# The down product of a conv-gated feed-forward network: Strassen-Winograd sums against eight open PSUM banks, and absorbed attention weights moved behind the token rows

## The chip, the cores and the metric

One core of one Trainium2 chip. The metric is device microseconds of the whole kernel, the median of the runs of one build. The engines are TensorE (PE), VectorE (DVE), ScalarE (ACT), GpSimd (POOL) and the queue SyncE (SP), which issues nearly all of this kernel's DMAs.

## What is computed

A decoder trunk of two layers over 1024 tokens of width 1024, in fp32. Layer 0 mixes tokens by an RWKV-7 recurrence, layer 1 by sparse attention (an indexer picks 256 keys per token); each is followed by a feed-forward network and both by a layer norm over a scaled residual. The parts that the change touches:

```python
def conv_ffn(x, w_up, conv_w, conv_b, w_down):       # w_down: (2816, 1024)
    u = x @ w_up
    u = sum(up[:, j:j + S] * conv_w[j] for j in range(CONV_W)) + conv_b
    gate, val = jnp.split(u, 2, axis=-1)
    return (jax.nn.silu(gate) * val) @ w_down
...
x = layer_norm(DN_ALPHA * x + f, ln_g[i, 1], ln_b[i, 1])

def dsa_attention(x, w_in, ..., w_uq, w_uk, ...):
    h = x @ w_in                                     # 456 columns
    ...
    q = (c_q @ w_uq).reshape(B, S, H, QK_HEAD)
    q_abs = jnp.einsum('bthd,hdc->bthc', q_b, w_uk)  # w_uq and w_uk are multiplied ahead ("absorbed")
```

## The kernel before, in words

`trunk` (line 1937) makes four generators: `rwkv` (307), `ffn` for layer 0 (884), `dsa` (1270), `ffn` for layer 1. `drive` (1945) steps two neighbours in turn, one `yield` each, so that the end of one phase and the start of the next stand side by side. Within that, the framework's scheduler sets each engine's order; engines wait for one another by semaphores, and buffers of a pool's tag are taken in turn.

An fp32 product is made of three fp32r matmuls: `split` (line 50) writes a cast `hi` (line 54, ScalarE) and the remainder `lo` (line 60, POOL or VectorE), and `mm3` (lines 63 to 67) multiplies hi by hi, and each hi by the other's lo. A matmul of the down product has 128 rows and 512 columns, and its result is one PSUM bank of 128 x 512.

The feed-forward network multiplies up, makes the gated convolution (`gated`, lines 1028 to 1049, mostly VectorE), and stores the hidden rows, transposed, as `hd` in DRAM: 22 blocks f of 128 hidden columns by 1024 tokens. The last two blocks are gated inside the down part.

The **down product** (lines 1124 to 1266) works on pairs of blocks by the seven products of Strassen and Winograd, named 11, 12, S1 to S4 and 22. The pairs are put into groups (cuts 0, 3, 6, 8, 10 in layer 0, and 0, 3, 6, 9 in layer 1). `d_load` (1135, 1136) loads hidden rows and weight rows of a pair; `d_op` (1143) makes the sums and differences `q` and `raw` on VectorE (908, 1147) and splits them into `dh` and `dl`; `down` does, for each of four token tiles tt, three matmuls per pair of the group into a bank `dn`. `add_to` (1164) reads the bank after every product step and adds it to `acc` in SBUF, 196 times over both layers (1166). Blocks left over, two in layer 0 and four in layer 1, are plain products `dt` (tiles `to`, `tr`) per token tile and half of the columns, read at line 1260, and followed by the layer norm and the store of the tile (`norm_store`, line 149 the store).

The attention's first steps are: `uq` and `uk` are loaded (1316, 1319) and multiplied in eight groups of fp32 matmuls of 64 rows (`wqk`, 1326); each result is copied (1330, ScalarE), split (`wqkh`, `wqkl`) and stored for later (1334). The input weights `w_in` come as eight blocks through two raw tiles (1339) and are split into `win`. Each token tile is then loaded (`x_load`, 1310, two halves `xr`), transposed (`x_T`, 1357, `pt`), cast, and projected (`w_in`, `win`: 24 matmuls of 456 columns), two tiles behind the loads. Then come the transposes `ht`, the indexer's weights (`wr`, `wq`, line 1456), its product `qi`, and the query blocks; a table `toep` of 1 MB (1466) takes the buffer of `uq`. Six shared buffers `u` hold `xr`, `uk`, `wqk`, `wqkl` and the normalised projections.

Of the kernel before, what the change touches and what calls it, by code (L numbers as in the profile page):

```python
# [7 lines left out]
F32 = mybir.dt.float32  # L8
# [6 lines left out]
D = 1024  # L15
# [868 lines left out]
def ffn(k, layer, src, dst):  # L884
# [239 lines left out]
    NPAIR = NF // 2  # L1124
    cuts = [0, 3, 6, 8, 10] if layer == 0 else [0, 3, 6, 9]
    groups = [range(a, b) for a, b in zip(cuts, cuts[1:])]
    in_P = (0, 3, 4, 8, 9) if layer == 0 else (0, 3, 6, 8)
    tail = range(2 * cuts[-1], NF)
    acc = []
    R = {}  # L1130

    def d_load(p):
        r = R[p] = dict(raw=big("raw", P_ if p in in_P else L_, (128, 8, 512), F32))
        raw = r["raw"]
        nc.sync.dma_start(raw[:, 0:4].rearrange("p (f a) c -> p f (a c)", f=2), hd[p].rearrange("f p c -> p f c"))
        nc.sync.dma_start(
            raw[:, 4:8].rearrange("p (f a) c -> p f (a c)", f=2),
            k.w_down[layer, p * 256 : (p + 1) * 256, :].rearrange("(f p) c -> p f c", p=128),
        )

    def d_op(p, n, pool, lo_eng):

        r = R[p]
        raw = r["raw"]
        if n == "S1":
            q = r["q"] = sm("q")
            nc.vector.tensor_tensor(q[:, 0], raw[:, 1], raw[:, 3], ALU.add)  # L1147
            sub(q[:, 1], raw[:, 5], raw[:, 4])
        elif n == "S2":
            q = r["q"]  # L1150
            sub(q[:, 0], q[:, 0], raw[:, 0])
            sub(q[:, 1], raw[:, 7], q[:, 1])
        elif n == "S3":
            sub(raw[:, 1:6:4], raw[:, 0:8:7], raw[:, 1:6:4])
        elif n == "S4":
            sub(raw[:, 2], raw[:, 2], r["q"][:, 0])
        elif n == "22":
            sub(raw[:, 6], raw[:, 6], r["q"][:, 1])
        hi, lo = t4("dh", F32R, pool, (128, 2, 512)), t4("dl", F32R, pool, (128, 2, 512))
        r[n] = hi, lo  # L1160
        at = {"11": slice(0, 5, 4), "12": slice(2, 7, 4), "S3": slice(1, 6, 4), "S4": slice(2, 8, 5), "22": slice(3, 7, 3)}
        split(k, raw[:, at[n]] if n in at else r["q"], hi, lo, "a", lo_eng)

    def add_to(hf, tt, ch, ps, first):
        o = acc[hf][:, tt, 512 * ch : 512 * ch + 512]
        nc.vector.scalar_tensor_tensor(o, o, ALPHA if first else 1.0, ps, ALU.mult, ALU.add)  # L1166

    B_ = {}

    def down(gi, n, tt):  # L1170
        new = n in ("11", "12", "S1")
        x = n in ("11", "S2", "S3", "22")
        if new:
            B_[x, tt] = bank("dn", PX if x else PY)
        ps = B_[x, tt]
        tsl = slice(128 * tt, 128 * tt + 128)
        for j, p in enumerate(groups[gi]):
            hi, lo = R[p][n]
            mm3(
                k, ps, (hi[:, 0, tsl], lo[:, 0, tsl]), (hi[:, 1], lo[:, 1]), new and j == 0,  # L1180
                n in ("12", "S4", "22") and j == len(groups[gi]) - 1, skip_group_check=True,
            )
        hf, ch = {"11": (0, 0), "12": (0, 0), "S1": (1, 1), "S2": (0, 1), "S3": (1, 1), "S4": (0, 1), "22": (1, 0)}[n]
        add_to(hf, tt, ch, ps, gi == 0 and n in ("11", "S1", "S2", "22"))

    for p in groups[0]:
        d_load(p)
    for hf in range(2):
        a = big("acc", L_, (128, 4, 1024), F32)
        acc.append(a)  # L1190
        for tt in range(4):
            nc.sync.dma_start(a[:, tt], src[(4 * hf + tt) * 128 : (4 * hf + tt + 1) * 128, :])
    ng = len(groups)
    dsteps = [(gi, n) for gi in range(ng) for n in ("11", "12", "S1", "S2", "S3", "S4", "22")]
    done = set()

    def d_ops(j):
        if j < len(dsteps) and j not in done:
            done.add(j)
            gi, n = dsteps[j]  # L1200
            for i, p in enumerate(groups[gi]):
                d_op(p, n, N_ if i == 2 else P_, CFG["dl0"][3 * j + i] if j < 3 else "v" if i == 2 and n in ("11", "12", "S4") else "p")

    hs = []

    def tail_op(f):

        if layer == 1 and f == NF - 1:
            room = [t4("to", F32R, N_) for _ in range(4)]
        else:  # L1210
            room = big("to", L_, (128, 4, 1024))
            room = [room[:, i] for i in range(4)]
        for i, ap in enumerate((hd[f // 2][f % 2], k.w_down[layer, f * 128 : (f + 1) * 128, :])):
            raw = t4("tr")
            nc.sync.dma_start(raw, ap)
            split(k, raw, room[2 * i], room[2 * i + 1], "a", "p")
        hs.append(room)

    late = [NF - CFG["gl"] + i for i in range(CFG["gl"])]
    for j, (gi, n) in enumerate(dsteps):  # L1220
        for x in CFG["ga"] if j == 0 else "":
            if x == "g":
                gated(late.pop(0))
            else:
                d_ops(int(x))
        d_ops(j)
        if n == "11" and gi + 1 < ng:
            for p in groups[gi + 1]:
                d_load(p)
        d_ops(j + 1)  # L1230
        if j == 0:
            while late:
                gated(late.pop(0))
        if gi == ng - 1 and n in ("S2", "S3", "S4") and (i := ("S2", "S3", "S4").index(n)) < len(tail):
            tail_op(tail[i])
        for tt in range(4):
            down(gi, n, tt)
    if len(tail) > 3:
        tail_op(tail[3])
    lnw = []  # L1240
    for z in range(2):
        if layer == 0:
            lnw.append(L_.tile([128, D], F32, name=f"lnw{z}"))
        else:
            lnw.append(sm("lnw").rearrange("p a b -> p (a b)"))
        i = B_LN + 4 * layer + 2 + z
        nc.sync.dma_start(lnw[z], k.bvec[i : i + 1, :].to_broadcast([128, D]))
    if layer == 0:
        pools.close(P_, N_, PY)
        yield  # L1250
    for tt in range(8):
        tsl = slice(128 * tt, 128 * tt + 128)
        r = [acc[tt // 4][:, tt % 4, 512 * ch : 512 * ch + 512] for ch in range(2)]
        sums = L_.tile([128, 2], F32, name="lns", tag="lns", bufs=2)
        for ch in range(2):
            cs = slice(512 * ch, 512 * ch + 512)
            ps = bank("dt")
            for i, (a, b, c, d) in enumerate(hs):
                mm3(k, ps, (a[:, tsl], b[:, tsl]), (c[:, cs], d[:, cs]), i == 0, i == len(hs) - 1)
            nc.vector.scalar_tensor_tensor(  # L1260
                r[ch], r[ch], 1.0, ps, ALU.mult, ALU.add, accum_out=sums[:, ch : ch + 1]
            )
# [713 lines left out]
```

## Time and profile before

| | us |
|---|---|
| median of 3 runs | 3173.01 (3172.37 to 3178.31) |
| profiled execution, own time | 3170.01 |
| its span, first to last instruction | 3168.0 |
| down product of layer 0, first `dn` to last `dt` | 1437.8 to 1729.6 |
| start of the attention up to the indexer's product | to 1784.65 |
| down product of layer 1 | 2893.1 to 3158.9 |

| engine | busy us | share of the span |
|---|---|---|
| PE | 2834.0 | 89% |
| DVE | 2463.5 | 78% |
| POOL | 1528.7 | 48% |
| ACT | 1368.9 | 43% |

The mean granted clock of TensorE is 0.937 of full speed. The spans of the table of engines overlap, so a share says little about one stage; the stages are read one by one, by their stretch of the span. "Idle before" in a row is what ended the engine's idle time ahead of it.

### The profile page before, as it was taken

To read this page: it belongs to the slowest core of one execution; us is meant where nothing else is said; L and a number is where in the kernel's file an instruction comes from. 1 tells how busy PE (TensorE), PEld (TensorE's weight loads), DVE (VectorE), ACT (ScalarE), POOL (GpSimd) and SP (SyncE) were. 2 spreads that over 40 slices of the span, in tenths; PEclk is the share of its full clock that TensorE was granted. 3 is DMA by queue.
4 is the path that set the end of the run, shared out by engine and by line. 5 is a ranking of instruction groups with operands and counts; after the bars stand their busy time and mean duration, and the time that the engine had idled before them with its cause. 6 is when DMAs were issued, how large, how long until landed. Compare 5 with 4: busy or idle time off the path is not lost. (4 is left out here: it accounts for less than half of the span.)

```text
span 3168.0 us, 41686 instructions
## 1 busy us (share of the span) xinstructions
PE 2834.0 (89%) x15032; PEld 2217.4 (70%) x15032; DVE 2463.5 (78%) x3911; ACT 1368.9 (43%) x2353; POOL 1528.7 (48%) x987
## 2 busy tenths in 40 slices
PE   7789998898988999997888888889998899998798
PEld 3577576786866777775667765667776677777577
DVE  6776776768576888889786699995675888888965
ACT  4433243322233544443224487784363444444231
POOL 3525045140246666666677222212214666666766
PEclk9889998898998999998998989899999999999899
DMA  6645435344162222244115221113224222225212
GB/s 214 246 152 195 142 121 199 134 148 146 64 201 89 80 80 80 80 143 189 41 40 173 102 90 37 34 40 115 77 66 151 60 80 80 80 81 206 80 53 93
DMA packets 235232, 354.87 MB, mean 112 GB/s; under 512 B 17194, under 2 KB 110762, under 8 KB 234642
## 3 DMA queue, kind: packets, MB, share of 16 engines
q1 hardware_dynamic: 221202, 327.04, 31.6%
q10 hardware_dynamic: 13824, 25.17, 2.2%
q8 instruction: 118, 1.93, 0.3%
q14 instruction: 88, 0.72, 0.1%
HBM read 248.99 MB, written 103.15 MB: 111 GB/s over the span
## 5 line engine op out<-in xcount | busy, mean ns | idle before, releaser
L60 POOL TENSOR_TENSOR wo<-wr,wo 128x512 fp32r<-128x512 f32 x220 | 414.3, 1907 | 289.4 <-ACT wo L54 289.4
L1039 DVE SCALAR_TENSOR_TENSOR cv<-u,vec,cv 128x1023 f32<-128x1023 f32 (+1 forms) x176 | 348.0, 1995 | 52.9 <-ACT cv L1034 51.2
L65 PE MATMUL dn<-dh 128*128 128x512 f32 x532 | 220.3, 414 | 67.8 <-DVE acc L1166 67.8
L60 POOL TENSOR_TENSOR dl<-raw,dh 128x1024 fp32r<-128x1024 f32 x82 | 220.2, 2708 | 102.2 <-ACT dh L54 96.7
L65 PE MATMUL p<-xT,wo 128*128 128x512 f32 x528 | 213.1, 404 | 27.8 <-ACT u L1023 18.2
L66 PE MATMUL dn<-dl,dh 128*128 128x512 f32 x532 | 218.1, 410 | 14.3 <-DVE dl L60 7.5
L1671 POOL TENSOR_TENSOR cm<-sc,toep 128x256 f32<-128x256 f32 x96 | 75.7, 795 | 298.1 <-DVE mn L1687 229.7
L1034 ACT ACTIVATE cv<-u,vec 128x1024 f32<-128x1024 f32 x88 | 109.5, 1244 | 250.2 <-DVE u L1028 249.6
L67 PE MATMUL dn<-dh,dl 128*128 128x512 f32 x532 | 217.0, 408 | 0.0
L67 PE MATMUL p<-xT,wo 128*128 128x512 f32 x528 | 208.8, 395 | 2.9 <-POOL wo L60 2.9
L66 PE MATMUL p<-xT,wo 128*128 128x512 f32 x528 | 208.5, 395 | 3.0 <-DVE xT L60 3.0
L1166 DVE SCALAR_TENSOR_TENSOR acc<-acc,dn 128x512 f32<-128x512 f32 x196 | 131.0, 680 | 86.3 <-PE dn L67 86.3
L60 POOL TENSOR_TENSOR wo<-S,wo 128x512 fp32r<-128x512 f32 x88 | 173.3, 1987 | 30.0 <-ACT wo L54 25.7
L54 ACT CAST dh<-raw 128x1024 fp32r<-128x1024 f32 x95 | 94.8, 1047 | 199.6 <-issue 81.1
L65 PEld LDWEIGHTS dn<-dh 128*128 128x128 f32 x532 | 106.3, 200 | 98.5 <-DVE acc L1166 42.2
L60 POOL TENSOR_TENSOR wl<-wr,wh 128x512 fp32r<-128x512 f32 x56 | 76.3, 1363 | 181.7 <-ACT wh L54 109.1
L65 PEld LDWEIGHTS p<-xT,wo 128*128 128x128 f32 x528 | 100.7, 191 | 65.4 <-ACT u L1023 33.0
L65 PE MATMUL p<-x,wo 128*128 128x512 f32 x352 | 138.9, 394 | 3.4 <-DVE x L60 3.0
L54 ACT CAST wo<-wr 128x512 fp32r<-128x512 f32 x220 | 127.2, 619 | 27.3 <-POOL wo L60 18.6
L67 PE MATMUL p<-x,wo 128*128 128x512 f32 x352 | 138.4, 393 | 0.0
L66 PE MATMUL p<-x,wo 128*128 128x512 f32 x352 | 138.4, 393 | 0.0
L66 PEld LDWEIGHTS dn<-dl,dh 128*128 128x128 f32 x532 | 106.5, 200 | 38.4 <-DVE dl L60 8.4
(412 smaller groups left out, 8552.0 us busy)
## 6 DMA issues: line engine op xcount, KB each, us to landing
wr<-in_w_up_dram SPq DMA_DIRECT2D x88, 512.0 KB, 5.9
hd<-cv SPq DMA_DIRECT2D x44, 512.0 KB, 3.4
raw<-hd SPq DMA_DIRECT2D x19, 1024.0 KB, 5.0
raw<-in_w_down_dram SPq DMA_DIRECT2D x19, 1024.0 KB, 7.6
wr<-in_w_wo_dram SPq DMA_DIRECT2D x68, 256.0 KB, 2.9
wr<-in_w_rkv_dram SPq DMA_DIRECT2D x48, 256.0 KB, 4.3
kept_w<-wh ACTq DMA_DIRECT2D x48, 256.0 KB, 3.5
kept_w<-wl SPq DMA_DIRECT2D x48, 256.0 KB, 3.0
```

The source lines that it names most:

```text
L54: nc.scalar.copy(hi, raw)
L60: eng.tensor_tensor(lo, raw, f32(hi), ALU.subtract)
L65: mm(ps, lhs[0], rhs[0], start=start, stop=False, **kw)
L66: mm(ps, lhs[0], rhs[1], start=False, stop=False, **kw)
L67: mm(ps, lhs[1], rhs[0], start=False, stop=stop, **kw)
L1034: nc.scalar.activation(o, u, AF.Identity, bias=k.vec[:, cb : cb + 1], scale=k.vec[:, cw[2] : cw[2] + 1])
L1039: nc.vector.scalar_tensor_tensor(o[:, d:], u[:, : 1024 - d], k.vec[:, cw[j] : cw[j] + 1], o[:, d:], ALU.mult, ALU.add)
L1166: nc.vector.scalar_tensor_tensor(o, o, ALPHA if first else 1.0, ps, ALU.mult, ALU.add)
L1671: (nc.vector if CFG["cm"][h4] == "v" else nc.gpsimd).tensor_tensor(cm[:, :near], mk, toep[g][:, h % 8, 256 - near :], ALU.add)
```

## The change

The down product is a plain one. Tokens are done in two halves hf of 512. For each pair p of hidden blocks `d_prep`, two steps ahead, loads half of the hidden rows (`hr`) and two blocks of the weights (`dr`), and splits all three; the weights are loaded and split anew for the second half. `d_mm` does six matmuls into each of eight banks (four token tiles by two halves of the columns), which stay open over all 11 pairs, 48 matmuls a step. The last two pairs are done bank by bank in `d_end`, which reads the bank once (line 1167 of the new file), and `d_norm` norms and stores the tile. The second half's last banks are taken in turn with the attention's first steps.

In the attention, the absorbed weights become a function `absorb`, called after the loop over token tiles; the rows of tiles 0 and 1 are loaded first; `w_in` comes through five raw tiles, two of tag `qr` and three of tag `ph`. Of the diff, the removed down product is cut out; it stands above.

```diff
-    cuts = [0, 3, 6, 8, 10] if layer == 0 else [0, 3, 6, 9]
...
+    NPAIR, LAST = NF // 2, 2
+    ops, hold, lnw, sums, rows = {}, {}, [], {}, {}
+    def d_prep(hf, p):
+        late = hf == 1 and p >= NPAIR - LAST
+        hr = t4("hr")
         nc.sync.dma_start(
+            hr.rearrange("p (f c) -> p f c", f=2), hd[p][:, :, 512 * hf : 512 * hf + 512].rearrange("f p c -> p f c")
         )
+        if late:
...
+            h = hold["h"][:, i], hold["h"][:, i + 1]
+        else:
+            h = t4("hh", F32R), t4("hl", F32R)
+        w = big("wd", L_ if late or layer and (hf * NPAIR + p) % 2 else P_, (128, 4, 1024))
+        split(k, hr, *h, "a", "p" if layer and hf and p < 4 else "v")
+        for f in range(2):
+            wr = t4("dr", pool=N_)
+            nc.sync.dma_start(wr, k.w_down[layer, (2 * p + f) * 128 : (2 * p + f + 1) * 128, :])
+            split(k, wr, w[:, 2 * f], w[:, 2 * f + 1], "a", "p")
+        ops[hf, p] = *h, w
+
+    def d_mm(ps, hf, p, tt, ch):
+        hh, hl, w = ops[hf, p]
+        for f in range(2):
+            ts = slice(512 * f + 128 * tt, 512 * f + 128 * tt + 128)
+            cs = slice(512 * ch, 512 * ch + 512)
             mm3(
+                k, ps, (hh[:, ts], hl[:, ts]), (w[:, 2 * f, cs], w[:, 2 * f + 1, cs]), p == f == 0,
+                p == NPAIR - 1 and f == 1,
             )
+    def d_end(ps, hf, tt, ch):
+        for p in range(NPAIR - LAST, NPAIR):
+            d_mm(ps, hf, p, tt, ch)
...
+        nc.vector.scalar_tensor_tensor(
+            r, r, ALPHA, ps, ALU.mult, ALU.add, accum_out=sums[hf, tt][:, ch : ch + 1]
+        )
+    def d_norm(hf, tt):
...
+    steps = [(hf, p) for hf in range(2) for p in range(NPAIR)]
+    for s in steps[:2]:
+        d_prep(*s)
+    for f in range(NF - CFG["gl"], NF):
+        gated(f)
+    order = [(ch, tt) for ch in (1, 0) for tt in range(4)]
+    for i, (hf, p) in enumerate(steps):
+        if i + 2 < len(steps):
+            d_prep(*steps[i + 2])
+        if p == 0:
+            bk = {x: bank("dn", PX if x[0] == 0 else PY) for x in order}
+        if p < NPAIR - LAST:
+            for ch, tt in order:
+                d_mm(bk[ch, tt], hf, p, tt, ch)
...
+        if (hf, p) == (0, NPAIR - 1):
+            for ch, tt in order:
+                d_end(bk[ch, tt], 0, tt, ch)
+                if ch == 0:
+                    d_norm(0, tt)
+    for tt in range(4):
+        d_end(bk[1, tt], 1, tt, 1)
     if layer == 0:
         pools.close(P_, N_, PY)
         yield
+        for tt in range(4):
+            yield
+    for tt in range(4):
+        d_end(bk[0, tt], 1, tt, 0)
+        d_norm(1, tt)
         if layer == 0:
             yield
...
+    def absorb():
+        uq = T_.tile([128, 8, 256], F32, name="uq", tag="toep", bufs=1)
+        nc.sync.dma_start(uq, k.w_uq.rearrange("p (h c) -> p h c", h=8))
+        for h4 in range(2):
+            uk = u("uk")
+            nc.sync.dma_start(uk, k.w_uk[:, 512 * h4 : 512 * h4 + 512])
...
+    for tt in range(2):
+        x_load(tt)
     win = []
     for kt in range(KT):
         wt = w4("win", (128, 2, 512), F32R)
-        raw = qr("wr")
+        raw = (ph_ if kt % 5 > 1 else qr)("wr")
...
     for tt in range(8):
-        x_load(tt)
+        if tt >= 2:
+            x_load(tt)
         if tt >= LAG:
             early(2)
         yield
+    absorb()
```

VectorE at the start of layer 0's down product. `acc<-acc,dn` is the accumulation of a bank, `q` and `raw` the sums of the seven products, `cv` the convolution of the leftover gated blocks. Before:

```order
L1039 SCALAR_TENSOR_TENSOR cv<-u_11285,vec,cv 128x1022
L1166 SCALAR_TENSOR_TENSOR acc<-acc,dn 128x512
L1048 TENSOR_TENSOR cv<-cv 128x1024
L60 TENSOR_TENSOR dl<-raw,dh 128x1024
L1166 SCALAR_TENSOR_TENSOR acc<-acc,dn 128x512 x2
L908 TENSOR_TENSOR q<-q,raw 128x512
L908 TENSOR_TENSOR q<-raw,q 128x512
L1166 SCALAR_TENSOR_TENSOR acc<-acc,dn 128x512
L908 TENSOR_TENSOR q<-q,raw 128x512
L1039 SCALAR_TENSOR_TENSOR cv<-u_11307,vec,cv 128x1023
L1166 SCALAR_TENSOR_TENSOR acc<-acc,dn 128x512
```

Now, with `hl<-hr,hh` the remainder of the hidden rows of a pair:

```order
L1039 SCALAR_TENSOR_TENSOR cv<-u_11285,vec,cv 128x1022
L1039 SCALAR_TENSOR_TENSOR cv<-u_11307,vec,cv 128x1023
L1048 TENSOR_TENSOR cv<-cv 128x1024
L1039 SCALAR_TENSOR_TENSOR cv<-u_11307,vec,cv 128x1022
L60 TENSOR_TENSOR hl<-hr,hh 128x1024
L1048 TENSOR_TENSOR cv<-cv 128x1024
L60 TENSOR_TENSOR hl<-hr,hh 128x1024 x11
L1167 SCALAR_TENSOR_TENSOR acc,lns<-acc,dn 128x512 x5
```

The accumulations and sums between the convolutions are gone; one subtraction per pair of blocks is left, then the reads of the finished banks.

SP around the load of `uk`. `x_6_80` and `x_7_81` are the stored token tiles 6 and 7 of the network's result, `tr` the leftover blocks, `wr<-in_w_in_dram` the raw input weights. Before:

```order
L1316 DMA uq<-in_w_uq_dram 128x2048
L1215 DMA tr<-hd_10_8002 128x1024
L1215 DMA tr<-in_w_down_dram 128x1024
L1215 DMA tr<-hd_10_8002 128x1024
L1215 DMA tr<-in_w_down_dram 128x1024
L1319 DMA uk<-in_w_uk_dram 128x512
L1339 DMA wr<-in_w_in_dram 128x456 x3
L1334 DMA wqk<-wqkh 128x512
L1334 DMA wqk<-wqkl 128x512
```

Now:

```order
L149 DMA x_6_80<-acc 128x512 x2
L1265 DMA xr<-x_6_80 128x512 x2
L149 DMA x_7_81<-acc 128x512 x2
L1265 DMA xr<-x_7_81 128x512 x2
L1276 DMA uk<-in_w_uk_dram 128x512
L1422 DMA c_13793<-in_c_dram 128x16
L1438 DMA wuv<-in_w_uv_dram 128x1024
L1291 DMA wqk<-wqkh 128x512
L1291 DMA wqk<-wqkl 128x512
```

The load of `uk` stood ahead of the input weights and of all token rows; now it stands behind the store and the reload of the last token tile.

TensorE at the absorbed weights. `pt<-ident,xr` are the transposes of a token tile (here tile 6), `win` a tile's projection. Before:

```order
L67 MATMUL dt<-to 128x512
L1326 MATMUL wqk<-uk,uq 128x128 x16
L65 MATMUL dt<-to 128x512
L66 MATMUL dt<-to 128x512
L67 MATMUL dt<-to 128x512
```

Now:

```order
L67 MATMUL win<-win,X 128x456
L1317 MATMUL pt<-ident,xr 128x128 x8
L1283 MATMUL wqk<-uk,uq 128x128 x32
L65 MATMUL win<-win,X 128x456
L66 MATMUL win<-win,X 128x456
```

The absorbed weights stood in two parts among the tail products of the down product, with `dt` on both sides; now all 32 stand together behind the transposes of tile 6, ahead of the projections that are left.

## Rows read from the trace of the kernel before

**Rows 1.** Busy time by stretch: start and end, length, engines (instructions), clock, DMA share, GB/s.

```profile
core 0: us, PE busy (x) PEld busy (x) DVE busy (x) ACT busy (x) POOL busy (x), PEclk, DMA share, GB/s
1437.80:1729.60 291.80, 241.22 (x1001) 192.94 (x999) 229.25 (x247) 96.78 (x123) 201.54 (x89) 0.90 0.26 92
1440.00:1500.00 60.00, 37.19 (x141) 28.80 (x140) 59.93 (x43) 20.62 (x21) 43.09 (x15) 0.86 0.33 125
...
2893.10:3158.90 265.80, 230.62 (x949) 186.39 (x947) 207.90 (x235) 75.95 (x78) 182.38 (x80) 0.92 0.23 84
...
3080.00:3158.90 78.90, 78.89 (x349) 64.98 (x347) 48.65 (x99) 19.00 (x20) 55.50 (x34) 1.00 0.26 97
```

**Rows 2.** Waits of TensorE, 1437.8 to 1693: total us, times, longest.

```profile
PE dn L65 <- DVE acc L1166: 38.2, 10, 13.2
```

**Rows 3.** Waits of TensorE, 2893 to 3116.

```profile
PE dn L65 <- DVE acc L1166: 29.6, 6, 13.8
```

**Rows 4.** Chain that ended last, behind a stop: start, length, what.

```profile
3014.41 0.43 PE dn L66
```

**Rows 5.** Timeline of TensorE, single instructions: start, length, line, operation.

```profile
1437.82 0.39 PE L65 MATMUL dn<-dh 128*128 128x512 f32 x1
...
1713.86 0.57 PE L1326 MATMUL wqk<-uk,uq 64*128 64x128 f32 x3 [3.62 <-DMA uk<-in_w_uk_dram]
...
1751.79 0.71 PE L1357 MATMUL pt<-ident,xr 128*128 128x128 f32 x5
...
1784.65 0.58 PE L67 MATMUL qi<-XTh,wq 128*128 128x256 f32 x1 [0.22 <-POOL wq L60]
...
2893.11 0.39 PE L65 MATMUL dn<-dh 128*128 128x512 f32 x1
...
3157.15 0.39 PE L67 MATMUL dt<-to 128*128 128x512 f32 x1
...
3158.51 0.39 PE L67 MATMUL dt<-to 128*128 128x512 f32 x1
```

**Rows 6.** Splits of the down product: shortest, median and longest ns, first and last start.

```profile
L60 POOL TENSOR_TENSOR dl<-raw,dh x82: 2345/2784/3394, 1419.8 to 3103.4; 128x1024 fp32r<-128x1024 f32 x82
...
L54 ACT CAST dh<-raw x95: 1032/1046/1057, 1417.5 to 3101.0; 128x1024 fp32r<-128x1024 f32 x95
```

**Rows 7.** DMA issues: count, KB each, median us from issue to landing.

```profile
raw<-in_w_down_dram SPq DMA_DIRECT2D x19, 1024.0 KB, 7.6
...
tr<-in_w_down_dram SPq DMA_DIRECT2D x6, 512.0 KB, 4.5
toep<-in_toep_dram SPq DMA_DIRECT2D x2, 1024.0 KB, 6.1
uk<-in_w_uk_dram SPq DMA_DIRECT2D x2, 256.0 KB, 4.0
```

**Rows 8.** Timeline of VectorE at the program's end.

```profile
3158.93 0.69 DVE L1260 SCALAR_TENSOR_TENSOR acc<-acc,dt 128x512 f32<-128x512 f32 x1 [0.33 <-PE dt L67]
...
3161.96 0.75 DVE L108 SCALAR_TENSOR_TENSOR acc<-acc,lnrs,lnw 128x512 f32<-128x512 f32 x1
```

**Rows 9.** Timeline of SP's queue around the last token tiles.

```profile
1710.16 0.42 SPq L1319 DMA_DIRECT2D uk<-in_w_uk_dram  x1
...
1748.61 0.39 SPq L149 DMA_DIRECT2D x<-acc  x1
...
1752.95 0.42 SPq L149 DMA_DIRECT2D x<-acc  x1
...
1758.31 0.80 SPq L1310 DMA_DIRECT2D xr<-x  x2
```

**Rows 10.** Tile acc, 1690 to 1750: the reads of the tail's banks.

```profile
L1260 DVE SCALAR_TENSOR_TENSOR acc<-acc,dt x16: 670/675/689, 1694.3 to 1735.7; 128x512 f32<-128x512 f32 x16
```

**Rows 11.** Tile wqk: the absorbed weights' copy, cast and subtraction.

```profile
L1330 ACT ACTIVATE wqk<-wqk x8: 575/588/598, 1696.7 to 1724.6; 128x512 f32<-128x512 f32 x8
L54 ACT CAST wqkh<-wqk x8: 600/605/622, 1697.7 to 1726.6; 128x512 fp32r<-128x512 f32 x8
...
L60 POOL TENSOR_TENSOR wqkl<-wqk,wqkh x8: 1278/1488/1742, 1698.4 to 1728.0; 128x512 fp32r<-128x512 f32 x8
```

More of the change, by code (lines that the diff above doesn't have):

```diff
@@ L1121, in ffn @@
             gated(f)
-    NPAIR = NF // 2
-    cuts = [0, 3, 6, 8, 10] if layer == 0 else [0, 3, 6, 9]
[L1126 to L1135, printed above, removed]
+    NPAIR, LAST = NF // 2, 2
@@ L1186, in ffn @@
[L1186 to L1247, printed above, removed]
+            hr.rearrange("p (f c) -> p f c", f=2), hd[p][:, :, 512 * hf : 512 * hf + 512].rearrange("f p c -> p f c")
+        )
@@ new lines, in d_prep @@
+        if late:
+            if not hold:
+                hold["h"] = big("hl", L_, (128, 4, 1024))
+            i = 2 * (p - NPAIR + LAST)
+            h = hold["h"][:, i], hold["h"][:, i + 1]
[7 more added lines that the diff above has]
+            split(k, wr, w[:, 2 * f], w[:, 2 * f + 1], "a", "p")
@@ new lines, in d_norm @@
+    def d_norm(hf, tt):
+        r = [rows[hf][:, tt, 512 * ch : 512 * ch + 512] for ch in range(2)]
+        kw = {} if layer else dict(
+            sums=sums[hf, tt], junk=L_.tile([128, 512], BF16, name="lnj", tag="lnj", bufs=1)
+        )
+        norm_store(
+            k, L_, r, lnw, dst, 128 * (4 * hf + tt), CFG["ln4"][layer] if (hf, tt) != (1, 3) else "pv", **kw
+        )
+    steps = [(hf, p) for hf in range(2) for p in range(NPAIR)]
[3 more added lines that the diff above has]
+        gated(f)
@@ new lines, in ffn @@
+    order = [(ch, tt) for ch in (1, 0) for tt in range(4)]
[7 more added lines that the diff above has]
+                d_mm(bk[ch, tt], hf, p, tt, ch)
+        if p == 4:
+            rows[hf] = big("acc", L_, (128, 4, 1024), F32)
+            for tt in range(4):
+                nc.sync.dma_start(rows[hf][:, tt], src[(4 * hf + tt) * 128 : (4 * hf + tt + 1) * 128, :])
+            for z in range(0 if lnw else 2):
+                if layer == 0:
+                    lnw.append(L_.tile([128, D], F32, name=f"lnw{z}"))
+                else:
+                    lnw.append(sm("lnw").rearrange("p a b -> p (a b)"))
+                i_ = B_LN + 4 * layer + 2 + z
+                nc.sync.dma_start(lnw[z], k.bvec[i_ : i_ + 1, :].to_broadcast([128, D]))
+        if (hf, p) == (0, NPAIR - 1):
[3 more added lines that the diff above has]
+                    d_norm(0, tt)
@@ L1250, in ffn @@
         yield
[L1251 to L1262, printed above, removed]
-        kw = {} if layer else dict(sums=sums, junk=L_.tile([128, 512], BF16, name="lnj", tag="lnj", bufs=1))
-        norm_store(k, L_, r, lnw, dst, 128 * tt, CFG["ln4"][layer] if tt < 7 else "pv", **kw)
+        for tt in range(4):
+            yield
+    for tt in range(4):
+        d_end(bk[0, tt], 1, tt, 0)
+        d_norm(1, tt)
         if layer == 0:
```

78 lines of the change are left out of this document (18 added, 60 removed).

## The prediction, made before the change was run

> **What bounds the kernel now.** I went from the table by stage to the waits, then to single rows. Two stages hold almost everything the change touches: the down product of layer 0 with the start of the attention behind it, and the down product of layer 1, which ends the program.
>
> The table of stretches gives the down stage of layer 0, from 1437.8 to 1729.6, 291.8 us, in which TensorE was busy for 241.2 at a mean clock of 0.90; from 1440 to 1500 VectorE was busy for 59.93 of 60 us and TensorE for only 37.19 [rows 1]. The down stage of layer 1 takes 265.8 us with TensorE busy for 230.6 at 0.92; its last 78.9 us, from 3080, run at clock 1.00 without a gap [rows 1]. The reader is to see that the same multiplications run with and without a gap in the same stage, so something else stops TensorE. The waits of TensorE name it: in layer 0 it waited ten times, 38.2 us in all, for the accumulation on VectorE (line 1166) [rows 2], in layer 1 six times, 29.6 us [rows 3]. After such a stop the chain of waits shows matmuls 0.43 us apart [rows 4] where the timeline shows six in 1.36 us, 0.2267 us each, between 3157.15 and 3158.51 [rows 5]: a stop costs its own length and then some matmuls at about half pace. So the stage is bound by TensorE where VectorE keeps up, and by VectorE's sums, differences and accumulations where it does not.
>
> **The change, part by part.**
>
> *More matmuls.* Per layer the new form has 22 x 16 x 3 = 1056 matmuls. Before, it was 840 + 96 = 936 in layer 0 and 756 + 192 = 948 in layer 1 (products and tail). That is 228 more, at 0.2267 us [rows 5] 51.7 us of pure TensorE time, all of it on the path. The Trainium skill, "TensorE: Matmul & The Clock Gate", section "Back-to-back issue gap", gives about 131 ns for a sustained matmul of 512 columns; by it the 228 would cost 30 us and a layer's down product 138. No stretch here comes near that figure (the trace has 227 ns in gapless rows), so the measured pace stands.
>
> *Fewer stops.* A layer's down product now takes 1056 x 0.2267 = **239.4 us** if TensorE never waits. Banks stay open over all of the 22 row blocks, so the 196 accumulations into SBUF and all the sums and differences on VectorE go; one read of a bank remains per output block. What is left per step of 48 matmuls (10.88 us): two weight subtractions on POOL at 2.35 to 3.39 us [rows 6], at most 6.8; three casts on ScalarE at 1.05, 3.1 us [rows 6]; one token subtraction on VectorE, at most 3.4. The loads are three blocks of 512 KB per step, 1.57 MB in 10.88 us or 145 GB/s, little above the 125 GB/s that the stretch from 1440 moved with a third of the DMA engines' time [rows 1]. A 512 KB block of w_down landed in 4.5 us, 1 MB in 7.6 [rows 7], and six raw tiles (three steps' worth) and three pairs of split tiles let them run two steps, 21.8 us, ahead. All of it lies under TensorE's 10.88 us; if that cover went, a step would grow to what rival B says. The second split of the weights for the second half of the tokens is in these numbers. At the start of the stage the leftover gated blocks on VectorE stand between the first two token subtractions and the third; the third is first needed 21.8 us after the start, and the convolutions that stood ahead of the accumulations before now delay only that. I price this at nothing; the bound from above is one stop of the longest kind seen, 13.2 us in layer 0 and 13.8 in layer 1 [rows 2, 3], and a gain is excluded, since TensorE's 239.4 already has no gap.
>
> *Layer 1.* First matmul 2893.11, last 3158.51 + 0.39 [rows 5]: 265.8 us become 239.4, 26.4 less. Against it stand about 2 us of small stops (between 0 and one average stop of this layer, 29.6 / 6 = 4.9 [rows 3]; nearer 0, as nothing on VectorE recurs) and a longer tail: the last four token tiles now end every 12 matmuls, 2.72 us, where they ended every 24 before. VectorE needs from the read at 3158.93 to the end of the scaling at 3162.71 3.8 us, with the other half's statistics 0.7 more and 0.4 of it waiting for POOL [rows 8], so about 4.0 per tile; three tiles lag 1.3 each, 4 us. Sum **-20**, between -26 and -5 (one long stop and the tail).
>
> *Layer 0 and the attention's start.* I follow it to the first matmul that needs the indexer weights in full, `qi` at 1784.65 [rows 5]: from there on the program is the same. Last matmul of the down product after the change: 1437.8 + 239.4, plus four input projections of 24 matmuls of 456 columns that now stand between the last banks (by columns 24 x 0.2267 x 456/512 = 4.85 each, 19.4), 48 transposes (five in 0.71 us [rows 5], 6.8) and 6 for waits on the rows and norms between them (a norm alone is longer, but the banks of the next tile cover it): 1709. Then the absorbed weights. Before, `uk` was issued at 1710.16 for its second half, and the matmuls started at 1713.86, 3.7 later [rows 5, 9]; all of it ran beside the tail products. Now the `uk` load stands on SP behind the store and the reload of token tile 7, absorb's 32 matmuls stand on TensorE ahead of the remaining projections, and its 16 operations on ScalarE ahead of the casts of tile 7's transposes. The last tile's norm took 12.9 us from the last read on VectorE (1735.7 [rows 10]) to the first store (1748.61), with a loaded POOL; I take 10.5. The second store to the reload took 5.4 us (1752.95 to 1758.31, and 0.8 for two) [rows 9]. So absorb starts at 1709 + 10.5 + 5.4 + 0.8 + 3.7 = 1729, and TensorE has only some 6 us of other work meanwhile.
>
> Absorb itself goes group by group: half of the six shared buffers are still held by the token tile and its normalised copy, so each of the eight groups runs copy 0.59, cast 0.605 and POOL's subtraction 1.49 [rows 11] in a row, 2.7 us, 21.5 in all, with one reload of `uk` at 4.0 in the middle [rows 7]. The 1 MB `toep` table takes the place of `uq` and lands 6.1 us after it [rows 7], ahead of the last subtraction on POOL; then the indexer weights are loaded and split (some 6 us, the loads being queued behind the last stores). Together 38 us after absorb's start: `qi` at 1767, where it was 1784.65. **-18**, between 0 (twenty microseconds more of serial waiting) and -35 (absorb hidden as before).
>
> *The rest.* Five raw tiles for w_in let its eight splits run further ahead, and loading rows 0 and 1 first moves loads that TensorE does not wait for; both at nothing, covered by the last steps of the down product, some 20 us. If that cover were gone, the two POOL subtractions and two casts ahead cost a few microseconds.
>
> *Sum.* The profiled execution took 3170.01 us: 3170 - 20 - 18 = 3132. The median of the three runs lies 3.0 above it, so the forecast is **3135**.
>
> **The rivals.**
> - *A, absorb's new place eats layer 0's gain.* For it: uk, its reload, toep and the indexer weights are all in one row on SP, and 38 us is a sum of medians without any queueing. It decides when the chain from absorb to `qi` is 56 us in place of 38. Then layer 0 gives 0 and the time is 3170 - 20 + 3 = 3153. Chance 0.18.
> - *B, slower: the doubled weight traffic is not hidden.* If a step's weights land, are cast and split in a row without overlap, it takes 7.6 + 1.05 + 3.39 = 12.04 us [rows 6, 7] where TensorE needs 10.88; 44 steps x 1.16 = 51 us, and the time is 3135 + 51 = 3186. The point from which it decides: the 38 us are used up at 0.86 us a step, a step over 11.75. For it: POOL holds half of the work and its subtraction varies by 1 us. Against: loads run two steps ahead and there are raw tiles for three steps. Chance 0.09.
> - *C, nothing is lost behind the products.* Layer 1 gives all 26, layer 0 all 35: 3170 - 61 + 3 = 3112. For it: the gapless last 78.9 us of [rows 1]. Chance 0.10.
> - *D, the clock falls although TensorE does not wait long.* All eight banks are visited in every step, six matmuls each; should small gaps between banks lower the clock, a matmul costs 0.43 in place of 0.2267 [rows 4, 5], and 190 matmuls of the 2112 at that pace use up the whole 38 us. Then it is no change, or slower: 3173 to 3190. The Trainium skill names such a thing, "TensorE: Matmul & The Clock Gate", section "A second HAM failure mode: psum-queue depth-cycling". Against it: the last 78.9 us of layer 1 go from bank to bank every 12 matmuls at clock 1.00 [rows 1]. Chance 0.03.
>
> **How the numbers follow.** My forecast's case has 0.60, A 0.18, C 0.10, B 0.09, D 0.03. A measurement of this kernel tells some 0.2%, 6.3 us, from no change: faster is below 3166.7, slower above 3179.4. Faster: 0.60, C's 0.10 and most of A, 0.15, give 0.85; the same: the end of A and a part of D, 0.04; slower: B and the rest of D, 0.11. The range runs from C's 3112 less a few microseconds for an earlier absorb, 3108, to 3170, where layer 0 gives nothing and layer 1 only a little; it leaves out B and D.
>
> **What would show it.** Right: 1056 matmuls per layer, the granted clock near 1.00 over both stages, the waits for line 1166 gone, each down stage near 240 us, `qi` near 1767, an idle stretch of TensorE of some 10 us ahead of the absorbed weights. Wrong: steps longer than 11 us with waits for POOL's subtraction or a w_down load (B); a `qi` at 1785 or later with down near 240 (A); a clock under 0.95 with no wait (D); a new wait of VectorE's queue at the start of the stage, which I priced at nothing.

## The result, and the profile after

The changed kernel took 3140.20 us (median of 4 runs, 3136.21 to 3152.14) where the kernel before took 3175.66 in the same comparison: 0.989 of it, 95% interval 0.9853 to 0.9926. Forecast were 3135 and a gain of 38 us; measured is a gain of 35.5. A second comparison gave 0.9871 (0.9845 to 0.9897).

The profiled execution is the longest of the four, 3152.14 us with a span of 3150.4, so only 17.6 us below the profiled execution before. Single rows say where. The timeline of TensorE after the change, first and last matmul of each down product and the steps between, which answers to [rows 5]:

```profile
1460.73 0.39 PE L65 MATMUL dn<-wd,hh 128*128 128x512 f32 x1
...
1727.57 0.39 PE L67 MATMUL dn<-wd,hl 128*128 128x512 f32 x1
...
1745.44 0.98 PE L1283 MATMUL wqk<-uk,uq 64*128 64x128 f32 x3 [9.99 <-DMA uk<-in_w_uk_dram]
...
1762.44 0.98 PE L1283 MATMUL wqk<-uk,uq 64*128 64x128 f32 x3 [10.52 <-DMA uk<-in_w_uk_dram]
...
1786.64 0.58 PE L67 MATMUL qi<-XTh,wq 128*128 128x256 f32 x1 [0.22 <-POOL wq L60]
...
2894.94 0.39 PE L65 MATMUL dn<-wd,hh 128*128 128x512 f32 x1
...
3134.08 0.39 PE L67 MATMUL dn<-wd,hl 128*128 128x512 f32 x1
```

Cut at these marks, the span falls into four stretches (`qi` is the first matmul that needs all of the indexer's weights; the fourth ends with the span):

| stretch | before | after | difference |
|---|---|---|---|
| start to layer 0's first `dn` | 1437.8 | 1460.7 | +22.9 |
| layer 0's first `dn` to `qi` | 346.8 | 325.9 | -20.9 |
| `qi` to layer 1's first `dn` | 1108.5 | 1108.3 | -0.2 |
| layer 1's first `dn` to the end | 274.9 | 255.5 | -19.4 |

The two stretches that the change touches give 40.3 us, half each. The first stretch, in which nothing was edited, lost 22.9 in this pair of executions; the experiments below show what that is.

Busy time by stretch, with [rows 1]'s columns, in the changed kernel:

```profile
1460.70:1786.60 325.90, 297.17 (x1352) 248.74 (x1350) 114.43 (x205) 116.28 (x183) 157.81 (x94) 0.94 0.47 163
1735.00:1769.00 34.00, 13.49 (x69) 12.79 (x67) 5.67 (x24) 10.64 (x22) 9.54 (x10) 0.54 0.51 171
2895.00:3134.50 239.50, 239.46 (x1057) 198.02 (x1055) 81.14 (x95) 70.05 (x71) 132.27 (x60) 1.00 0.44 159
3134.50:3150.40 15.90, 0.00 (x0) 0.00 (x0) 7.64 (x18) 2.44 (x3) 8.54 (x8) 0.58 0.31 116
```

The third row is the clearest: layer 1's down product is 239.5 us in which TensorE never stops, at clock 1.00, with VectorE busy for a third of it. Before, the same stage was 265.8 us with VectorE busy for 207.9 [rows 1]. The waits of TensorE for the accumulations [rows 2, 3] have no successor there. What is left in layer 0 is in the second row, 34 us with 13.5 of TensorE work at clock 0.54, and one row of TensorE's waits (1440 to 1800) says for what:

```profile
PE wqk L1283 <- DMA uk<-in_w_uk_dram: 20.5, 2, 10.5
```

SP's queue in that place, which answers to [rows 9], shows the load of `uk` behind the store and the reload of token tile 7, and the second half of it behind the store of the fourth group:

```profile
1737.42 2.63 SPq L149 DMA_DIRECT2D x<-acc  x2
1740.17 1.98 SPq L1265 DMA_DIRECT2D xr<-x  x2
1742.19 0.42 SPq L1276 DMA_DIRECT2D uk<-in_w_uk_dram  x1
...
1758.68 0.32 SPq L1291 DMA_DIRECT2D wqk<-wqkl  x1
1759.10 0.39 SPq L1276 DMA_DIRECT2D uk<-in_w_uk_dram  x1
```

The splits of the weights (shortest, median, longest ns) and their load, which answer to [rows 6, 7]:

```profile
L54 ACT CAST wd<-dr x88: 1034/1051/1058, 1450.2 to 3092.0; 128x1024 fp32r<-128x1024 f32 x88
L60 POOL TENSOR_TENSOR wd<-dr,wd x88: 2379/2404/3395, 1451.4 to 3094.5; 128x1024 fp32r<-128x1024 f32 x88
```

```profile
dr<-in_w_down_dram SPq DMA_DIRECT2D x88, 512.0 KB, 3.6
```

### The profile page after: what moved, and what is told of

Same layout as the page of the kernel before. It is cut to its first block, busy times and chain, and to the rows that moved or that the text cites. A ratio compares the mean times of both kernels' runs of the same rounds, so it can differ in the third digit from the quotient of the medians.

```text
span 3150.4 us, 41855 instructions
## 1 busy us (share of the span) xinstructions
PE 2866.6 (91%) x15260; PEld 2255.0 (72%) x15260; DVE 2169.2 (69%) x3609; ACT 1359.9 (43%) x2340; POOL 1407.7 (45%) x947
## 4 chain that ended last, share of the span: by engine, by line
PE 30%; DVE 20%; issue 6%; ACT 5%; POOL 3%; DMA 2%; SPq 0%; POOLq 0%; ACTq 0%; DVEq 0%
DVE cv L1039 8%; PE dn L66 4%; PE dn L67 4%; PE dn L65 4%; DVE cj L1526 2%; PE p L65 2%; DVE S L908 2%; PE p L66 2%; PE p L67 2%; ACT cv L1034 1%; DVE p L1649 1%; ACT wo L54 1%; PE pS L67 1%; PE pS L65 1%; PE pS L66 1%
## 5 line engine op out<-in xcount | busy, mean ns | idle before, releaser
L60 POOL TENSOR_TENSOR wd<-dr,wd 128x1024 fp32r<-128x1024 f32 x88 | 223.9, 2566 | 136.1 <-ACT wd L54 136.1
L67 PE MATMUL dn<-wd,hl 128*128 128x512 f32 x704 | 274.0, 389 | 0.0
L65 PE MATMUL dn<-wd,hh 128*128 128x512 f32 x640 | 249.0, 389 | 0.0
L66 PE MATMUL dn<-wd,hh 128*128 128x512 f32 x640 | 249.0, 389 | 0.0
L60 DVE TENSOR_TENSOR hl<-hr,hh 128x1024 fp32r<-128x1024 f32 x36 | 59.2, 1644 | 160.2 <-ACT hh L54 103.2
L67 PEld LDWEIGHTS dn<-wd,hl 128*128 128x128 f32 x704 | 132.2, 188 | 27.1
L65 PE MATMUL p<-x,wo 128*128 128x512 f32 x352 | 138.4, 393 | 3.3 <-DVE x L60 2.9
L66 PEld LDWEIGHTS dn<-wd,hh 128*128 128x128 f32 x640 | 120.2, 188 | 25.1
L65 PEld LDWEIGHTS dn<-wd,hh 128*128 128x128 f32 x640 | 120.2, 188 | 25.0
L54 ACT CAST wd<-dr 128x1024 fp32r<-128x1024 f32 x88 | 89.4, 1050 | 112.5 <-DMA dr<-in_w_down_dram 50.2
L66 PE MATMUL p<-x,wo 128*128 128x512 f32 x352 | 137.6, 391 | 0.0
```

What stands on the lines that cost most here:

```text
L54: nc.scalar.copy(hi, raw)
L60: eng.tensor_tensor(lo, raw, f32(hi), ALU.subtract)
L65: mm(ps, lhs[0], rhs[0], start=start, stop=False, **kw)
L66: mm(ps, lhs[0], rhs[1], start=False, stop=False, **kw)
L67: mm(ps, lhs[1], rhs[0], start=False, stop=stop, **kw)
```

## The experiments

All of them are read by the same four marks. "First" is the time of layer 0's first `dn`, "layer 0" from there to `qi`, "middle" to layer 1's first `dn`, "layer 1" from there to the end of the span, each from one profiled execution; the ratio to the kernel before is of medians of several runs, each to runs of the kernel before in the same comparison. Rows without a ratio were run once, and only their stretches are read.

| kernel | first | layer 0 | middle | layer 1 | ratio |
|---|---|---|---|---|---|
| before | 1437.8 | 346.8 | 1108.5 | 274.9 | 1 |
| before_again | 1451.2 | 348.1 | 1108.6 | 273.8 | |
| after | 1460.7 | 325.9 | 1108.3 | 255.5 | 0.989 (0.9853 to 0.9926) |
| after_again | 1462.0 | 326.6 | 1109.0 | 255.4 | 0.9871 (0.9845 to 0.9897) |
| l1_only | 1444.6 | 347.1 | 1110.2 | 255.4 | 0.9922 (0.9895 to 0.9949) |
| old_dsa | 1461.9 | 313.2 | 1108.2 | 255.5 | 0.983 (0.9798 to 0.9862) |
| uk_early_in4 | 1459.7 | 304.2 | 1106.0 | 255.5 | 0.9805 (0.9776 to 0.9834) |
| absorb_in4 | 1446.6 | 313.0 | 1107.0 | 255.5 | |
| two_raw | 1447.0 | 327.9 | 1108.1 | 255.4 | |
| rows_late | 1456.0 | 327.4 | 1106.4 | 255.4 | |
| tail_rows | 1456.0 | 325.9 | 1108.2 | 248.6 | |
| pool_twice | 1440.0 | 380.8 | 1106.9 | 299.6 | |
| best | 1452.6 | 303.1 | 1107.1 | 248.7 | 0.9789 (0.9764 to 0.9815) |
| best2 | 1466.7 | 304.9 | 1106.6 | 248.7 | 0.9793 (0.9747 to 0.9838) |

**The stretch that nobody edited.** The changed kernel and the kernel before, each once more, unedited.

> The changed kernel once more, for its scatter. The profile of the change had 1460.7 us up to the first matmul of layer 0's down product where the kernel before had 1437.8, with more of that stretch at half clock, although nothing there was edited; the three stretches behind it were 325.9 (down product of layer 0 to the indexer's full weights), 1108 (attention and layer 1's up product) and 255.7 us (layer 1's down product to the end). Theory: those three are the kernel's own and return within 2 us, and the first stretch is scatter of the clock: it comes out anywhere from 1435 to 1462, and the time with it. Rival: the change slows the recurrence itself, and the first stretch is 1458 to 1463 again.

> The kernel before once more, for the stretch up to the first matmul of layer 0's down product. It was 1437.8 us in the first profile of this kernel and 1444.6 with the new down product in layer 1 alone, but 1459.7 to 1462.0 in four profiles with the new down product in layer 0, by more time at half clock in the recurrence, whose instructions are the same. Theory: scatter, an untouched kernel can show 1450 to 1465 as well. Rival: the change in layer 0 lengthens the recurrence, and this kernel stays at 1437 to 1447. The other stretches: 346 to 348, 1107 to 1111, 274 to 276.

The three later stretches of the changed kernel came back within 0.7 us. The first was 1462.0 again, which spoke for the rival; the kernel before had 1451.2 in its second profile, outside the rival's band. Two kernels with the new layer 0 settle it: pool_twice, 1440.0, and best2, 1466.7. The rows of that stretch in four kernels, in the order before, after, pool_twice, best2:

```profile
0.00:1437.80 1437.80, 1305.70 (x8088) 1006.51 (x8089) 1083.26 (x1368) 557.87 (x902) 650.53 (x445) 0.94 0.43 142
```

```profile
0.00:1460.70 1460.70, 1325.66 (x8088) 1023.65 (x8089) 1075.57 (x1362) 557.62 (x901) 647.07 (x444) 0.92 0.42 137
```

```profile
0.00:1440.00 1440.00, 1307.94 (x8088) 1008.60 (x8089) 1077.91 (x1361) 555.48 (x899) 648.88 (x445) 0.93 0.43 138
```

```profile
0.00:1466.70 1466.70, 1332.54 (x8088) 1029.45 (x8089) 1074.86 (x1362) 557.88 (x901) 645.94 (x444) 0.92 0.42 136
```

The same 8088 matmuls in the same order; what differs is TensorE's busy time and its mean clock. To compare one place, the same matmuls must be cut out, for the executions drift apart. The 2301st to the 2500th, in the recurrence, took 13.2 us before at clock 1.00 and 19.0 after, of which 13.6 at 0.50, the lower of the clock's two levels (1.2 in place of 2.4 GHz):

```profile
421.20:434.40 13.20, 13.20 (x207) 11.37 (x205) 10.01 (x13) 6.37 (x11) 3.37 (x3) 1.00 0.47 160
```

```profile
424.90:443.90 19.00, 19.00 (x206) 16.17 (x203) 10.00 (x13) 6.34 (x11) 3.37 (x3) 0.64 0.32 111
427.00:440.60 13.60, 13.60 (x119) 11.37 (x121) 5.51 (x6) 3.67 (x7) 2.85 (x2) 0.50 0.35 120
```

In both TensorE was busy without a gap (the counts take in a few neighbours that reach into the window). best2 has the long form of this place (19.0), pool_twice the short one (13.2). l1_only, whose layer 0 is the old one, has the long form of another: the 3601st to the 3800th took 18.4 us at clock 0.50 in it and 18.5 at 0.50 in the changed kernel, where the kernel before and pool_twice took 13.8 and 13.9 at 0.75.

So the first stretch scatters with the clock it is granted, by 27 us over the kernels with the new layer 0 and by 13 over the three profiles with the old one, and 23 us of it hid more than half of the gain in the first pair of profiles. The profiles alone don't exclude that the kernels with the new layer 0 lie higher on average. The timed medians bound it: behind the first stretch after, old_dsa, uk_early_in4, best and best2 are 40.5, 53.3, 64.5, 71.3 and 70.0 us shorter than the kernel before, and their medians lie 35.5 (41.3 in the second comparison), 52.3, 60.8, 69.3 and 61.6 below its median. What is left for the first stretch is 3 us on average and 8 at most, not 23. What decides when the recurrence falls to the lower clock was not tried.

**Do the layers add up?** The new down product in layer 1 alone, the old one kept as a second function:

```diff
+    yield from (down_plain() if layer == 1 else down_sums())
```

> The new down product in layer 1 alone; layer 0 and the attention's start as before. Theory (the two layers give their gains separately): layer 1's last stretch 255 to 257 us in place of 274.9, layer 0's 346 to 348 as before, the time 19 us below the kernel before, 0.994 of it. Rival: layer 1's gain needs the other edits or is less, above 0.997.

Layer 1 gave its 19.5 us alone and layer 0 stayed; 0.9922 is 25 us of 3182, with an interval that takes in the 19. The layers are separate.

**Where the absorbed weights cost.** First the attention's start as it was before, with the new down product in both layers:

```diff
-    def absorb():
...
-    for tt in range(2):
-        x_load(tt)
...
+    uq = T_.tile([128, 8, 256], F32, name="uq", tag="toep", bufs=1)
...
-        raw = (ph_ if kt % 5 > 1 else qr)("wr")
+        raw = qr("wr")
...
-    absorb()
```

> The new down product in both layers, with the attention's start as before (absorbed weights ahead of the input weights, two raw tiles, rows loaded after). Theory: the place of the absorbed weights behind tile 7's reload costs layer 0 the two waits for uk, 20.5 us in the changed kernel; in the old place the 32 matmuls lie among the last banks, and the stretch from layer 0's first down matmul to the indexer's full weights is 302 to 310 us in place of 325.9. Rival: the chain of the last token tile (norm, store, reload, transposes) sets the indexer's start anyway, 320 or more. Second rival: two raw tiles delay the input weights so far that it is slower than the change, over 330.

313.2: neither in my band nor the rival's. Two waits of TensorE in it:

```profile
PE pt L1311 <- DMA xr<-x: 12.1, 1, 12.1
PE wqk L1280 <- DMA uk<-in_w_uk_dram: 2.5, 1, 2.5
```

The wait for `uk` went from 20.5 to 2.5 as the theory has it, but one for the first token rows took 12.1 of it back. SP's queue shows why: the loads of the rows stand behind the stores of all eight groups of absorbed weights, here the last of them, and behind `grow`:

```profile
1721.87 0.32 SPq L1288 DMA_DIRECT2D wqk<-wqkl  x1
1722.30 0.39 SPq L1297 DMA_DIRECT2D grow<-in_dsa_rows_dram  x1
1722.74 9.17 SPq L1264 DMA_DIRECT2D xr<-x  x10
```

The new start of the attention is thus 12.7 us worse than the old one behind the same down product: that part of the change costs time. Then the place of the absorbed weights alone, with `uk` as it is in the change:

```diff
         if tt >= LAG:
             early(2)
+        if tt == 4:
+            absorb()
         yield
-    absorb()
```

> The change with the absorbed weights computed behind token tile 4's loads, uk still taking turns in the six shared buffers and loaded where they are computed. Theory (what costs is that uk's load stands behind the last tile's reload): one place earlier is enough for most of it, the stretch from layer 0's first down matmul to the indexer's full weights 304 to 314 us in place of 325.9, with a wait for uk under 8 us left. Rival (the shared buffers are what holds uk back, since the second uk waits for the fourth group and the token rows now take its place): two waits of some 10 us stay, and the stretch is 320 or more.

The stretch fell to 313.0, inside the theory's band, but the waits left are 13.3 us, more than it allowed, and one is still of 10.6:

```profile
PE wqk L1283 <- DMA uk<-in_w_uk_dram: 13.3, 2, 10.6
```

So the reload of tile 7 ahead of `uk` on SP is one part of the cost: the first wait is down from 9.99 to 2.7. The long wait that is left is for the second half of `uk`. The rival puts it down to the six shared buffers, but no wait of SP for such a buffer stands ahead of that load, here or in the changed kernel; it is issued right behind the last store of the fourth group, as there:

```profile
1716.01 0.32 SPq L1291 DMA_DIRECT2D wqk<-wqkl  x1
1716.44 0.40 SPq L1276 DMA_DIRECT2D uk<-in_w_uk_dram  x1
```

What holds it back is thus its place in SP's queue, behind a store that waits for the fourth group's subtraction. Whether the buffers alone would have held it was not tried. With both halves of `uk`, and `uq`, loaded ahead of the token tiles, into the two tiles `qr` (issued at 1687.4 and 1688.7, used from 1705.8 on), and absorb behind tile 4 as in absorb_in4:

```diff
-        uq = T_.tile([128, 8, 256], F32, name="uq", tag="toep", bufs=1)
-        nc.sync.dma_start(uq, k.w_uq.rearrange("p (h c) -> p h c", h=8))
...
-            uk = u("uk")
-            nc.sync.dma_start(uk, k.w_uk[:, 512 * h4 : 512 * h4 + 512])
+            uk = uks[h4]
...
+    uq = T_.tile([128, 8, 256], F32, name="uq", tag="toep", bufs=1)
+    nc.sync.dma_start(uq, k.w_uq.rearrange("p (h c) -> p h c", h=8))
+    uks = [qr("uk") for _ in range(2)]
+    for h4 in range(2):
+        nc.sync.dma_start(uks[h4], k.w_uk[:, 512 * h4 : 512 * h4 + 512])
...
+        if tt == 4:
+            absorb()
         yield
-    absorb()
```

> The change with uk loaded ahead of the token tiles into the two raw tiles of the input weights, and the absorbed weights computed behind token tile 4's loads. Theory: both waits for uk go, the stretch from layer 0's first down matmul to the indexer's full weights falls from 325.9 to 303 to 310 us, about 18 us of the time. Rival: the eight groups' serial chain of copy, cast and subtraction, or the last tile's norm and reload, takes the place of the waits, and the stretch stays over 318.

304.2, 21.7 us less, and no row for `uk` is left among TensorE's waits; the longest is now this one:

```profile
PE pt L1319 <- DVE hn L1354: 2.7, 1, 2.7
```

The two waits, 20.5 us, were what absorb's new place cost, with `uk` loaded where it is used, and nothing of their size took their place.

**The parts priced at nothing.** Two raw tiles for the input weights, and the first rows loaded late:

```diff
-        raw = (ph_ if kt % 5 > 1 else qr)("wr")
+        raw = qr("wr")
```

> The change with the input weights through two raw tiles again, all else as in the change. Theory (priced at nothing, since the last banks of layer 0 cover the eight loads and splits): the stretch from layer 0's first down matmul to the indexer's full weights stays at 325 to 328 us. Rival: the splits come late for the first projection and it grows by 5 us or more.

```diff
-    for tt in range(2):
-        x_load(tt)
     win = []
...
-        if tt >= 2:
-            x_load(tt)
+        x_load(tt)
```

> The change with rows 0 and 1 loaded in the loop over token tiles again, behind the input weights. Theory (priced at nothing): the same stretch stays at 325 to 328 us. Rival: TensorE waits for the first rows behind the last banks, as in the kernel with the old attention start, where it waited 12.1 us for xr, and the stretch is 333 or more, or the wait only moves and it stays.

327.9 and 327.4: each is worth at most 2 us where the change has it. The 12.1 us for `xr` in old_dsa therefore don't come from the late rows alone, nor from the two raw tiles alone; in rows_late no store of absorbed weights stands ahead of the rows on SP. The late rows and two raw tiles together, without those stores, were not tried.

**The tail of layer 1.** The last four tiles finished one by one:

```diff
-    for tt in range(4):
-        d_end(bk[1, tt], 1, tt, 1)
+    if layer == 0:
+        for tt in range(4):
+            d_end(bk[1, tt], 1, tt, 1)
...
     for tt in range(4):
+        if layer:
+            d_end(bk[1, tt], 1, tt, 1)
         d_end(bk[0, tt], 1, tt, 0)
```

> The change with layer 1's last four token tiles finished tile by tile (both halves of the columns, 24 matmuls, then the norm) in place of all first halves, then all second halves. Theory: the last tiles come every 5.4 us in place of 2.7, VectorE keeps up, the end behind the last matmul shrinks from 16.3 us to 9 to 11, and layer 1's last stretch from 255.5 to 249 or 250 us. Rival: the end is set by the store and the last tile's own norm, and the stretch stays above 254.

248.6: the change's order of the last banks cost 6.9 us. The timeline of the changed kernel's end shows the pace. It was not VectorE's own work that set it but the order on POOL's queue: each tile's power (line 103, 0.54) stood behind the tile before's last addition (line 111), and line 104 on VectorE waited for it:

```profile
3137.31 1.59 POOL L111 TENSOR_TENSOR acc<-acc,lnw 128x512 f32<-128x512 f32 x1
3138.86 0.54 POOL L103 TENSOR_TENSOR lnrs<-lnve,mhalf 128x1 f32<-128x1 f32 x1
3139.44 0.16 DVE L104 SCALAR_TENSOR_TENSOR lnnm<-lnmv,lnrs 128x1 f32<-128x1 f32 x1 [1.66 <-POOL lnrs L103]
...
3140.12 0.73 DVE L108 SCALAR_TENSOR_TENSOR acc<-acc,lnrs,lnw 128x512 f32<-128x512 f32 x1
...
3144.29 0.74 DVE L108 SCALAR_TENSOR_TENSOR acc<-acc,lnrs,lnw 128x512 f32<-128x512 f32 x1
```

The two scalings of line 108 are 4.2 us apart, and the one ahead of them (3135.38) 4.7, where 24 matmuls take 5.4.

**How much cover the weight splits have.** Every subtraction of a weight block made twice:

```diff
             split(k, wr, w[:, 2 * f], w[:, 2 * f + 1], "a", "p")
+            nc.gpsimd.tensor_tensor(w[:, 2 * f + 1], wr, f32(w[:, 2 * f]), ALU.subtract)
```

> The change with each subtraction of a weight block made twice on POOL (the same result written again). POOL's work per step goes from 2 x 2.57 = 5.1 to 10.3 us beside TensorE's 10.88. Theory (the split lies under the matmuls): the stretches of both layers grow by less than 15 us each, 326 to 341 and 255 to 271. Rival (weights land, are cast and split in a row with the matmuls): 5.1 us more in each of 22 steps, over 100 us per layer.

My theory falls here: layer 0 grew by 54.9 us and layer 1 by 44.1, three to four times what I allowed, and about half of the rival's. Layer 0's first 240 us, the waits of TensorE in them and those of SP's queue:

```profile
1440.00:1680.00 240.00, 210.20 (x870) 168.68 (x868) 99.73 (x68) 77.48 (x89) 218.67 (x90) 0.95 0.44 151
```

```profile
PE dn L66 <- POOL wd L1148: 26.1, 12, 6.2
```

```profile
SPq L1146 <- POOL wd L1148: 134.4, 32, 8.2
```

POOL was busy for 218.7 of 240 us, so it had become all but the bound. Its work in them (how often, busy time, mean ns):

```profile
L1148 POOL TENSOR_TENSOR wd<-dr,wd 128x1024 fp32r<-128x1024 f32 x39 | 109.2, 2816 | 0.7
L60 POOL TENSOR_TENSOR wd<-dr,wd 128x1024 fp32r<-128x1024 f32 x39 | 98.9, 2550 | 10.2 <-ACT wd L54 10.2
```

A pair of subtractions took 5.37 us, so a step's four took 10.7 and not 10.3, and beside them the norms of the first half's tiles took 15.6 us of the same queue: the sum 10.3 under 10.88 left out the norms and every wait. And the raw tiles are held longer, so SP stood 134.4 us before loads of `dr`, with the hidden rows behind them in the queue (ScalarE waited 87.0 us for those). In the changed kernel these are 73.3 and 38.2 us between 1461 and 1680, and TensorE has no wait there. TensorE's stops brought lower clock besides: a mean of 0.95, and 210.2 us for 870 matmuls, some 13 more than at 0.2268 us each. The split's cover in the change itself is real, for no wait for `wd` shows there, but it is not the factor of two that 5.1 against 10.88 suggests: of the 5.6 us a step that the second subtractions took there, 2.5 came through in layer 0, and in layer 1 2.0 a step (54.9 and 44.1 over 22 steps).

**Together.** The early `uk` with the absorbed weights behind tile 4, and the last tiles one by one; then the same with the absorbed weights behind tile 2 (one number in the edit above).

> uk loaded ahead, the absorbed weights behind token tile 4, and layer 1's last tiles finished tile by tile. Theory: the two gains add, 304 us from layer 0's first down matmul to the indexer's full weights and 249 to 250 from layer 1's first down matmul to the end; the time some 6 us below the kernel with the early uk alone, 25 to 27 below the change, 0.978 of the kernel before. Rival: one of them is given back, 3120 us or more.

> As the fastest kernel so far (early uk, layer 1's last tiles one by one), with the absorbed weights behind token tile 2's loads in place of tile 4's. Theory: no wait for them is left in either, so the stretch from layer 0's first down matmul to the indexer's full weights is the same within 3 us, 300 to 306, and the time within 0.3%. Rival: the earlier place takes shared buffers from the token rows, and the stretch grows to 308 or more.

Both gains add: 303.1 and 248.7, and 0.9789 of the kernel before, 3113.26 against 3182.56 us. The rows of its two stages:

```profile
1452.60:1755.70 303.10, 293.60 (x1353) 244.04 (x1351) 115.60 (x205) 114.44 (x181) 158.01 (x94) 0.98 0.52 174
2862.80:3111.50 248.70, 239.54 (x1057) 198.01 (x1055) 90.09 (x113) 72.62 (x75) 140.71 (x67) 0.99 0.45 161
```

TensorE is busy for 293.6 of 303.1 us in the first of them. Behind tile 2 the stretch is 304.9, the time the same.

## Why the prediction was right, point by point

- *More matmuls for fewer stops.* 1056 matmuls took 239.53 us in layer 1, from 2894.94 to 3134.08 + 0.39; the prediction's term was 239.4. The pace is 0.2268 us each. The Trainium skill, "TensorE: Matmul & The Clock Gate", section "Back-to-back issue gap", has about 131 ns for a matmul of 512 columns in a sustained stream; the gapless stage here does not bear that out, and a forecast by it would have put each layer 101 us too low.
- *The price of nothing at the start of the stage* held: TensorE has no row among its waits from 1437 to 1710 in the changed kernel.
- *Layer 1.* Forecast 20, measured 19.4. Two sizes were off and cancelled: the stops, put at 2, were 0, and the tail, put at 4, was 6.8 (15.9 us behind the last matmul, 9.1 before). That the sum came out is luck in this part; what was off is "so about 4.0 per tile": the pace was that of POOL's queue, up to 4.7.
- *Layer 0.* Forecast 18, measured 20.9. To the last down matmul 267.2 where I had 271.2 (the 6 us of waits between the last tiles were 2). From there to the absorbed weights 17.5 where I had 20.4: 9.5 to the first store in place of 10.5, 2.3 more to the second, which the sum left out, 2.5 from there to the issue of `uk` in place of 6.2, and 3.3 to the first matmul in place of 3.7. The 10.5 was near for another reason than the one given: VectorE took up the last bank's read only at 1732.85, 4.9 us behind the last matmul, behind other work in its queue, and the norm from that read to the store took 4.6, not 10.5. From the absorbed weights to `qi` 41.2 where I had 38: the first four groups and the second load of `uk` 17.0 in place of 14.8, the second four groups 14.8 in place of 10.8, and from their last subtraction to `qi` 9.4 in place of 12.1, because the load of `toep`, issued at 1768.95, ran beside the groups. The idle TensorE, forecast at 10 us ahead of absorb, was there (9.99), and came a second time in its middle (10.5). That second wait was not foreseen as one of TensorE, but it is in the sum: 3.3 of it is the load of `uk` from issue to matmul, priced at 4.0, and the rest is the fourth group's own chain.
- *The rivals.* A did not happen, but its place is real: absorb's place, with `uk` loaded where it is used, cost 21.7 us that uk_early_in4 gives back. B did not happen; pool_twice shows that it was nearer than its chance of 0.09 was argued from. D did not happen: layer 1's 239.5 us cycle through eight banks at clock 1.00. The Trainium skill, "TensorE: Matmul & The Clock Gate", section "A second HAM failure mode: psum-queue depth-cycling", tells of a kernel that cycles through banks, idles for moments between groups and so swings between the clock's two levels; that is not seen here, where no idle moment stands between the groups. C's layer 1 came true for the matmuls and not for the tail.
- *The sum.* 3135 forecast, 3140.2 measured. Of the 5.2 us, 2.7 lie in the kernel before, whose median is 3175.66 here and was 3173.01 when the forecast was made; the gain is 35.5 in place of 38, and 41.3 in the second comparison. The 40.3 us of the two stages lie between, 2 more than forecast. Differences of this size are within the scatter of the first stretch, which the prediction's 0.2% for telling a change did not allow for.

## What to carry to other kernels

A form with a tenth fewer multiplications (936 against 1056) can lose to the plain one when its sums run on an engine with less to spare: compare the stage's length with the count of matmuls times their gapless pace before counting multiplications saved. When work moves in a program, follow each of its loads on the queue that issues it, and what stands ahead of it there; here two loads, one behind a store and a reload, one behind the store of a result still being made, cost 20 us of a stage that was otherwise full. Cut two profiles at marks that both have before explaining their difference: a stretch that nobody edited can hide half of it. Inside such a stretch compare the same instructions, not the same times.

## What the runs showed of the hardware that was not expected

The stretch up to the first `dn`, with the same matmuls in the same order, took between 1437.8 and 1466.7 us in 14 profiles, with a mean granted clock between 0.94 and 0.92. The difference lies in a few places of the recurrence in which one execution has the full clock and another half of it for some 10 us or more (the 2301st to 2500th matmul: 13.2 us at 1.00, or 19.0 with 13.6 of it at 0.50), TensorE being busy without a gap in both. Doubling POOL's subtraction, from 5.1 to 10.7 us a step beside 10.88 us of matmuls, was not hidden: it cost 54.9 and 44.1 us.
